# A two-layer decoder trunk on one core: the adaptive norms' parameters computed at other places, and an overflow branch moved

## The chip, the core and the metric

The kernel runs on one core of a Trainium2 chip. Five engines work side by side, each in its own order: TensorE (PE in the profile) multiplies matrices, VectorE (DVE) and ScalarE (ACT) work element by element, GpSimd (POOL) does little here, and SyncE (SP) issues the transfers from memory. The metric is the device time of one execution in microseconds; before the change its median is 909.39 us over 3 runs (909.15 to 909.47).

## What is computed

256 tokens of 1024 features pass through two layers. Each layer has a token mixer and a channel mixer, and each of the four sub-layers is wrapped in an adaptive norm whose parameters come from one vector c.

```python
def adaln_params(c, w, b):
    m = jax.nn.silu(c) @ w + b
    shift, scale, gate = jnp.split(m, 3, axis=-1)
    return shift[:, None, :], scale[:, None, :], gate[:, None, :]
...
    for i in range(DEPTH):
        shift, scale, gate = adaln_params(c, ada_w[i, 0], ada_b[i, 0])
        h = x * (1.0 + scale) + shift
        if i % N_MIXERS == 0:
            y = stick_breaking_attention(h, sb_w_in[i // 2], sb_w_out[i // 2])
        else:
            y = retention(h, positions, ret_w_in[i // 2], ret_gn_g[i // 2], ret_w_out[i // 2])
        x = layer_norm(DEEPNORM_ALPHA * x + (1.0 + gate) * y, ln_g[i, 0], ln_b[i, 0])
        shift, scale, gate = adaln_params(c, ada_w[i, 1], ada_b[i, 1])
        h = x * (1.0 + scale) + shift
        y = grouped_moe(h, router_w, router_b, moe_w_gate[i], moe_w_up[i], moe_w_down[i])
        x = layer_norm(DEEPNORM_ALPHA * x + (1.0 + gate) * y, ln_g[i, 1], ln_b[i, 1])
```

Layer 0 mixes tokens by stick-breaking attention (16 heads of 64), layer 1 by retention. The channel mixer routes every token to 2 of 16 experts; each expert computes silu(t @ w_gate) * (t @ w_up) @ w_down with 512 hidden features. All weights are float32: ada_w holds 4 x 1024 x 3072 of them, the experts of one layer 16 x 3 x 1024 x 512.

## The kernel before

**Stages.** The program runs through attention (the phase called STICK, 0 to about 207 us), the experts of layer 0 (SPARSE, to about 443 us), retention (RETEN, to about 660 us), the experts of layer 1 and the last norm. Nearly all bytes are weights. They come in tiles of 1 MB over one queue: SyncE issues them in program order into a ring of places, and an issue waits until the earlier owner of its place has been read. So a transfer that stands early in that order delays all behind it.

**Precision.** In the attention and retention products each float32 tile is split into a rounded part and a remainder (ScalarE L382, VectorE L383), and each product is three matmuls (L403 to L405). In the expert stages the matmuls take float32 as it is (L969 for gate and up, L1086 for down).

**Adaptive norms.** The parameters of sub-layer i are six parts j of 512 columns (shift 0 and 1, scale 2 and 3, gate 4 and 5). A part needs two ada_w tiles and is made in `ada_part`, on TensorE (L277) or by one multiply and seven multiply-adds on VectorE (L280, L282). Its rest, a turn into columns by four small matmuls (L292) and an addition of the bias (L293), comes later. `plan(i, js, on_pe)` puts parts on a list, each `fill()` finishes the last part and begins the next, `flush()` works the list off.

```python
    plan(0, range(4), on_pe=True)
...
    plan(2, range(1))
    plan(2, range(1, 4), on_pe=True)
```

**The start.** Four parts of norm 0 are made on TensorE, with the small tables (`vectors()`, L200 to L210) queued behind the first two tiles. Then x comes, is transposed (L448), shaped by the norm and split (`modulated`), and the dense products of q, k and v for the first half of the heads begin. `stick_attn` follows per pair of heads: z (L616, L617), a mask (DVE L619), three activations (ACT L621 to L623), a sum over keys on TensorE (L627, L628), an exponential (L630) and the product with v (L634, L635).

**The step to the experts.** After the output product of the attention layer come the logits of the router (L335, L343), the choice of experts, and the first gather of tokens (L940). In the program the last three parts of norm 2 stand between the output product and the logits.

**The experts.** Experts are worked in 8 pairs p: `up` for gate and up, `spread`, the gather of the next pair, the down products, and a scatter back (L1062) that is held over to the next pair. Each pair needs 12 tiles. An expert has room for a fixed number of tokens; `spill` handles those that overflow, inside a branch (L862) that all engines test and that is not taken with this input. It stands at the end of pair 1, behind the held scatter.

**The order.** Within each engine instructions run in a fixed order that a scheduler lays down when the program is built, from priorities (`urgent()` raises them) and from `tc.issue_after`; `behind(work)` puts work after the last matmul noted. On the chip an engine never passes over an instruction that waits.

## Time and profile before

| | |
|---|---|
| median of 3 runs | 909.39 us |
| the profiled execution: its own time, its span | 911.27 us, 909.6 us |
| TensorE busy | 854.3 us (94%) |
| VectorE busy | 500.6 us (55%) |
| ScalarE busy | 278.4 us (31%) |
| bytes moved | 310.05 MB, 341 GB/s over the span |

The profiled execution is one execution of the program. Its own time is 1.7 us above its span and 1.9 us above the median of the runs. A busy share is a mean over stages with different limits, so stages are read one by one: by windows, by the order of the instructions, and by who waited for whom.

### The profile page before, as it was taken

How to read it: one execution, taken by the hardware profiler on the slowest of the kernel's cores; microseconds unless marked ns; L12 is line 12 of the kernel's file. 1: busy time of each engine (PE TensorE's matmuls, PEld its weight loads, DVE VectorE, ACT ScalarE, POOL GpSimd, SP SyncE). 2: the span in 40 equal slices, each digit the busy share in tenths (PEclk: the TensorE clock that was granted, in tenths of full speed). 3: DMA queues.
4: the chain of work that ended last, by engine and by line, in shares of the span. 5: the costliest groups of instructions: out<-in, count | busy, mean ns of one | idle time of the engine just before them, and what ended most of it. 6: DMA issues, size and time to landing. Idle time of an engine off the chain costs nothing. (4 is left out here: it accounts for less than half of the span.)

```text
span 909.6 us, 11176 instructions
## 1 busy us (share of the span) xinstructions
PE 854.3 (94%) x4345; PEld 525.2 (58%) x4345; DVE 500.6 (55%) x943; ACT 278.4 (31%) x395; POOL 25.3 (3%) x46
## 2 busy tenths in 40 slices
...
GB/s 303 385 387 387 340 327 318 274 410 213 418 413 411 419 419 415 416 418 390 198 218 365 305 301 212 340 147 310 291 182 402 415 417 418 414 417 419 418 335 46
DMA packets 90035, 310.05 MB, mean 341 GB/s; under 512 B 5652, under 2 KB 6092, under 8 KB 73588
## 3 DMA queue, kind: packets, MB, share of 16 engines
...
HBM read 308.17 MB, written 1.05 MB: 340 GB/s over the span
## 5 line engine op out<-in xcount | busy, mean ns | idle before, releaser
L969 PE MATMUL ps<-s,xg 128*64 128x512 f32 x632 | 168.2, 595 | 2.2 <-DVEq L862 1.4
L969 PE MATMUL ps<-w,xg 128*64 128x512 f32 x392 | 111.7, 604 | 6.4 <-PEq L862 6.4
L969 PEld LDWEIGHTS ps<-s,xg 128*64 128x64 f32 x632 | 52.9, 137 | 86.5 <-issue 80.3
L1086 PE MATMUL ps<-w,hidT 128*64 128x512 f32 (+1 forms) x296 | 83.6, 574 | 0.1
L382 ACT ACTIVATE wp<-w 128x1024 fp32r<-128x1024 f32 x57 | 59.9, 1057 | 65.9 <-PE ps L405 59.4
L383 DVE TENSOR_TENSOR wp<-w,wp 128x1024 fp32r<-128x1024 f32 x57 | 69.3, 1218 | 18.2 <-ACT wp L382 18.2
L1019 DVE TENSOR_TENSOR mosg<-mosg,ps 128x512 f32<-128x512 f32 x16 | 11.0, 687 | 117.4 <-PE ps L969 117.4
L969 PEld LDWEIGHTS ps<-w,xg 128*64 128x64 f32 x392 | 35.7, 139 | 62.7 <-issue 60.7
L1086 PE MATMUL ps<-s,hidT 128*64 128x512 f32 (+1 forms) x248 | 71.8, 568 | 0.0
L282 DVE SCALAR_TENSOR_TENSOR s<-w,cact,s 128x512 f32<-128x512 f32 x88 | 65.6, 745 | 0.7
L1051 DVE SCALAR_TENSOR_TENSOR moy<-ps,cs,gate 128x512 f32<-128x512 f32 (+1 forms) x34 | 24.3, 716 | 71.8 <-PE ps L1086 71.8
L382 ACT ACTIVATE moyh<-moy 128x512 fp32r<-128x512 f32 (+1 forms) x34 | 20.6, 605 | 124.1 <-DVE moy L1051 124.1
L404 PE MATMUL ps<-wp,hh 128*128 128x512 f32 (+1 forms) x144 | 56.2, 392 | 0.0
L405 PE MATMUL ps<-wp,hl 128*128 128x512 f32 x144 | 55.5, 390 | 0.0
L454 ACT ACTIVATE xg<-ps,mod 128x256 f32<-128x256 f32 x32 | 17.8, 563 | 121.1 <-PE ps L940 121.1
L403 PE MATMUL ps<-wp,hh 128*128 128x512 f32 (+1 forms) x144 | 53.7, 393 | 0.6 <-ACT hh L382 0.6
L1067 DVE TENSOR_TENSOR res<-res,ps 128x512 f32<-128x512 f32 x48 | 30.4, 682 | 37.6 <-PE ps L1062 37.1
L1086 PEld LDWEIGHTS ps<-w,hidT 128*64 128x64 f32 x296 | 27.4, 136 | 33.9 <-issue 30.9
L1017 ACT ACTIVATE mosg<-ps 128x512 f32<-128x512 f32 x16 | 9.5, 596 | 112.3 <-PE ps L969 112.3
L1086 PEld LDWEIGHTS ps<-s,hidT 128*64 128x64 f32 x248 | 24.8, 137 | 29.9 <-issue 28.5
L403 PE MATMUL ps<-s,wp 128*128 128x256 f32 x128 | 37.6, 297 | 0.6 <-DVE fcol L222 0.6
L404 PE MATMUL ps<-s,wp 128*128 128x256 f32 x128 | 37.1, 293 | 0.0
(344 smaller groups left out, 1532.6 us busy)
## 6 DMA issues: line engine op xcount, KB each, us to landing
s<-in_moe_w_up SPq DMA_DIRECT2D x45, 1024.0 KB, 15.1
w<-in_ada_w SPq DMA_DIRECT2D x39, 1024.0 KB, 7.6
w<-in_moe_w_down SPq DMA_DIRECT2D x35, 1024.0 KB, 13.4
s<-in_moe_w_gate SPq DMA_DIRECT2D x34, 1024.0 KB, 11.6
w<-in_moe_w_gate SPq DMA_DIRECT2D x30, 1024.0 KB, 15.1
s<-in_moe_w_down SPq DMA_DIRECT2D x29, 1024.0 KB, 17.0
w<-in_moe_w_up SPq DMA_DIRECT2D x19, 1024.0 KB, 16.3
w<-in_ret_w_in SPq DMA_DIRECT2D x18, 1024.0 KB, 6.9
```

Of the source, the lines that this page charges most:

```text
L282: V.scalar_tensor_tensor(e, wt[:, kk, :], cact[:, k:k + 1], e, op0=OP.mult, op1=OP.add)
L382: A.activation(hi, src, AF.Copy)
L383: return V.tensor_tensor(lo, src, hi, op=OP.subtract).ins
L403: T.matmul(dst, lh, rh, start=start, stop=False)
L404: T.matmul(dst, lh, rl, start=False, stop=False)
L405: state["mm"] = T.matmul(dst, ll, rh, start=False, stop=stop).ins
L454: return A.activation(dst, src, AF.Identity, scale=sc[:, k:k + 1], bias=sh[:, k:k + 1]).ins
L969: state["mm"] = T.matmul(o[64 * u:64 * u + 64, :], xg[:, k, at:at + CAP], ts[u][kk], start=(k == 0), stop=(k == NK - 1)).ins
L1019: V.tensor_tensor(sgt, sgt, pu, op=OP.mult)
L1051: V.scalar_tensor_tensor(y, py, cs, gate[:, c0:c0 + n], op0=OP.mult, op1=OP.mult)
L1067: V.tensor_tensor(r, r, sos[b], op=OP.add)
L1086: state["mm"] = T.matmul(py[64 * u:64 * u + 64, :], hidT[:, f, u * CAP:(u + 1) * CAP], ts[h][u][:, i, c0:c0 + n], start=(f == 0), stop=(f ...
```

## The change

Four things change. First, norm 0 is made in two halves of the features: parts 0 and 2 and half of x come first, the first halves of the q and k products run on them (`feat_part`), and parts 1 and 3, the other half of x and the second halves follow. The small tables (`vectors()`, `folded_vectors()`, `aux`) are loaded behind that, out of `small_loads`; positions and router_b come as rows and are turned by TensorE. Second, the four parts of norm 2 leave the attention stage: they are planned for the expert stage of layer 0, one `fill()` after each of the pairs 1 to 5, all on VectorE. Third, `spill` moves from the end of pair 1 to the middle of pair 0 in both expert stages, and the expert tiles are loaded by `fetch` in an order of their own, 18 of them ahead of the branch. Fourth, in the expert stage the gathers and the last down products are put behind the last matmul noted, and the last moments become urgent.

```diff
...
 SLOTS = 8
+AHEAD = 18
...
-       "SPARSE": {"xs": (4, 1024), "xq": (2, 2048), "t2": (6, 512), "oneh": (2, 512), "pc": (1, 256), "pt": (2, 256)}}
+       "SPARSE": {"xs": (4, 1024), "xq": (2, 2048), "t2": (6, 512), "oneh": (2, 512), "pc": (1, 256), "pt": (2, 256), "E": (1, 512)}}
 HIGH = {"STICK": {"hA": (0, 1), "qz": ((2, 0), (3, 0)), "k4": ((4, 0), (4, 1024), (5, 0), (5, 1024)),
...
     A.activation(cact, colp[:, 0:8], AF.Silu)
+    col = keep([P, 176], "col")
+    adac = ps()
+    T.transpose(adac[:, 0:96], rows[0:96, 0, :], ident[0:96, 0:96])
+    V.tensor_copy(col[:, 0:96], adac[:, 0:96])
     part = keep([P, 2], "part")
...
         SY.dma_start(rows[64:80, 1, :], ret_gn_g[0].rearrange("(k p) -> k p", p=P))
         cq = ps()
-        T.transpose(cq[:, 0:96], rows[0:96, 0, :], ident[0:96, 0:96])
-        T.transpose(cq[:, 96:176], rows[0:80, 1, :], ident[0:80, 0:80])
-        V.tensor_copy(col, cq[:, 0:176])
+        T.transpose(cq[:, 0:80], rows[0:80, 1, :], ident[0:80, 0:80])
+        V.tensor_copy(col[:, 96:176], cq[:, 0:80])
         SY.dma_start(con[:, 2 * P:_KEPT], const[:, 2 * P:_KEPT])
-        SY.dma_start(posi, positions[0].rearrange("(b p) -> p b", p=P))
+        prow = big([P, 2, P], "rows")
+        posr = prow[0:NB, 0, :].bitcast(I32)
+        SY.dma_start(posr, positions[0].rearrange("(b p) -> b p", p=P))
+        SY.dma_start(prow[0:1, 1, 0:NE], router_b.rearrange("(o e) -> o e", o=1))
         SY.dma_start(wr.rearrange("p (t q) e -> p t q e", q=4), router_w.rearrange("(t p q) e -> p t q e", p=P, q=4))
-        SY.dma_start(rb, router_b.rearrange("(o e) -> o e", o=1).to_broadcast([P, NE]))
+        pr = ps()
+        prf = big([P, P], "crow")[0:NB, :]
+        V.tensor_copy(prf, posr)
+        T.transpose(pr[:, 0:NB], prf, ident[0:NB, 0:NB])
+        T.matmul(pr[:, NB:NB + NE], ones[0:1, :], prow[0:1, 1, 0:NE], start=True, stop=True)
+        V.tensor_copy(posi, pr[:, 0:NB])
+        V.tensor_copy(rb, pr[:, NB:NB + NE])
         V.tensor_copy(counts[:, 0, :], C["strict"])
...
-            for kk, wh, wl in pieces(w[kt * 512:(kt + 1) * 512, j * 512:(j + 1) * 512]):
-                k = 4 * kt + kk
-                for m in range(4):
-                    mm3(out_ps[m // 2][:, m % 2, :], wh[:, m * P:(m + 1) * P], wl[:, m * P:(m + 1) * P],
-                        hh[:, k, :], hl[:, k, :], k == 0 and m % 2 == 0, k == NK - 1 and m % 2 == 1)
+    def feat_part(out_ps, hh, hl, w, j, kt, amid=None):
+        for kk, wh, wl in pieces(w[kt * 512:(kt + 1) * 512, j * 512:(j + 1) * 512]):
+            k = 4 * kt + kk
+            if kk == 2 and amid:
+                amid()
+            for m in range(4):
+                mm3(out_ps[m // 2][:, m % 2, :], wh[:, m * P:(m + 1) * P], wl[:, m * P:(m + 1) * P],
+                    hh[:, k, :], hl[:, k, :], k == 0 and m % 2 == 0, k == NK - 1 and m % 2 == 1)
...
-        def whole(w, p, kt):
-            return [[t[:, f, :] for f in range(4)] for t in
-                    (load(w[l, 2 * p + u, 512 * kt:512 * kt + 512, :].rearrange("(p f) c -> p (f c)", p=P), None)
-                     for u in range(2))]
+        tiles, order = {}, [(w, p, h, u) for p in range(NE // 2) for w in range(3) for h in range(2) for u in range(2)]
+
+        def fetch(key=None, n=0):
+
+            while (key is not None and key not in tiles) or len(tiles) < n:
+                w, p, h, u = order[len(tiles)]
+                e = 2 * p + u
+                tiles[w, p, h, u] = load(moe_w_down[l, e, 256 * h:256 * h + 256, :], shape=(P, 2, 1024)) if w == 2 else \
+                    load((moe_w_gate, moe_w_up)[w][l, e, 512 * h:512 * h + 512, :].rearrange("(p f) c -> p (f c)", p=P), None)
+            return tiles.get(key)
...
                 held.pop(0)()
             sgt = big([P, 512], "mosg")
             A.activation(sgt, pg, AF.Silu)
-            pu = up(moe_w_up, p, xg, 1, up(moe_w_up, p, xg, 0))
+            pu = up(1, p, xg, 1, up(1, p, xg, 0))
             V.tensor_tensor(sgt, sgt, pu, op=OP.mult)
+            if p == 0:
+                fetch(n=AHEAD)
+                spill(l, xh, xl, sc, sh, over, flag, gate)
             pt, cs = spread(p, oneh)
...
-            if ahead:
+            if ahead and p:
+                behind(lambda: gather(nxt, 2 * (p % 2)))
+            elif ahead:
...
                         down(py, c0, w, h)
                 for py, (c0, w) in zip(pys, blocks):
                     weighed(py, c0, w)
-            if p == 1:
-                while held:
-                    held.pop(0)()
-                spill(l, xh, xl, sc, sh, over, flag, gate)
             after(p)
-    plan(0, range(4), on_pe=True)
+
+    def banks(tag):
+        t = ps([P, 2, 512], tag)
+        return [t[:, u, :].rearrange("p (m s) -> p m s", m=2) for u in range(2)]
+
+    plan(0, (0, 2), on_pe=True)
     fill()
-    vectors()
-    fill(2)
-    SY.dma_start(res, xrows)
-    aux = big([P, 5 * P], "aux")
+    SY.dma_start(res[:, :, 0:512], xrows[:, :, 0:512])
     fill()
-    SY.dma_start(aux, const[:, _KEPT:])
+    xT = banks("px")
+    for k2 in range(2):
+        transposed([res[:, b, :] for b in range(NB)], k2, xT[k2])
     flush()
     sc, sh = ada_mod(0)
-    hh, hl, _ = modulated([res[:, b, :] for b in range(NB)], sc, sh)
+    hh = big([P, NK, S], "hh", F32R)
+    hl = big([P, NK, S], "hl", F32R)
+
+    def shape_half(half, tps):
+        for k2, tp in zip((2 * half, 2 * half + 1), tps):
+            h = big([P, 2, S], "hm")
+            for q in range(2):
+                shaped(h[:, q, :], tp[:, q, :], sc, sh, 2 * k2 + q)
+            split_to(hh[:, 2 * k2:2 * k2 + 2, :], hl[:, 2 * k2:2 * k2 + 2, :], h)
+
+    shape_half(0, xT)
+    q0, k0 = banks("pz"), banks("px")
+    plan(0, (1, 3), on_pe=True)
+    feat_part(q0, hh, hl, sb_w_in[0], 0, 0)
+    SY.dma_start(res[:, :, 512:1024], xrows[:, :, 512:1024])
+    fill()
+    feat_part(k0, hh, hl, sb_w_in[0], 2, 0, fill)
+    xT = [transposed([res[:, b, :] for b in range(NB)], k2) for k2 in (2, 3)]
+    with urgent():
+        flush()
+        shape_half(1, xT)
     A.activation(res, res, AF.Copy, scale=ALPHA)
-    folded_vectors()
+    aux = big([P, 5 * P], "aux")
     plan(0, range(4, 6))
     plan(1, range(6))
-    plan(2, range(1))
-    plan(2, range(1, 4), on_pe=True)
     oh = big([P, NK, S], "oh", F32R)
     ol = big([P, NK, S], "ol", F32R)
+
+    def tables():
+        if small_loads:
+            small_loads.pop(0)()
+        fill()
+
+    small_loads = [lambda: SY.dma_start(aux, const[:, _KEPT:]), lambda: (vectors(), folded_vectors())]
     for half in range(2):
-        qkv = stick_in(hh, hl, half, fill)
+        qkv = stick_in(hh, hl, half, fill if half else tables, *(() if half else (q0, k0)))
         stick_attn(oh, ol, aux, *qkv, half)
     fill(2)
     gate = gate_row(0)
...
     st = stats_tiles(4)
-    moe(0, 1, xs, sc, sh, L, st, lambda p: rotary_tables() if p == 4 else None)
+    plan(2, range(4))
+    moe(0, 1, xs, sc, sh, L, st, lambda p: rotary_tables() if p == 6 else fill() if p else None)
+    flush()
     phase("RETEN", "second")
...
     moe(1, 3, xs, sc, sh, L, st, lambda p: rows_.append(ln_rows(3)) if p == NE // 2 - 1 else None)
-    for b, (m, r) in enumerate(both_moments(st)):
+    with urgent():
+        ends = both_moments(st)
+    for b, (m, r) in enumerate(ends):
```

VectorE in the attention stage, at the place where the norm's last features are shaped; before (L453 shapes them into s_207 and s_135, the L383 row with s_201 splits them, L282 works on a part of another norm):

```order
L280 TENSOR_SCALAR s_82<-s_376,cact 128x512
L282 SCALAR_TENSOR_TENSOR s_82<-s_376,cact,s_82 128x512
L453 TENSOR_SCALAR s_207<-ps_221,sums_101 128x256
L282 SCALAR_TENSOR_TENSOR s_82<-s_376,cact,s_82 128x512
L453 TENSOR_SCALAR s_135<-ps_230,sums_101 128x256
L282 SCALAR_TENSOR_TENSOR s_82<-s_376,cact,s_82 128x512
L383 TENSOR_TENSOR s_201<-s_207,s_200 128x512
L282 SCALAR_TENSOR_TENSOR s_82<-w_382,cact,s_82 128x512
L383 TENSOR_TENSOR s_201<-s_135,s_200 128x512
L383 TENSOR_TENSOR wp_314<-lo_312,wp_314 128x1024
```

And now, where L470 is the shaping of the second half of the features, L291 and L293 a part of another norm, L223, L209 and L218 copies of small tables, and L304 and L307 the end of part 3 of norm 0:

```order
L291 TENSOR_SCALAR s_82<-w_413,cact 128x512
L394 TENSOR_TENSOR wp_377<-s_348,wp_377 128x1024
L293 SCALAR_TENSOR_TENSOR s_82<-w_413,cact,s_82 128x512
L304 TENSOR_TENSOR sums_104<-ps_327,col 128x4
L223 CAST counts<-con 128x128
L293 SCALAR_TENSOR_TENSOR s_82<-w_413,cact,s_82 128x512
L307 TENSOR_SCALAR sums_104<-sums_104 128x4
L209 COPY col<-ps_488 128x80
L293 SCALAR_TENSOR_TENSOR s_82<-w_413,cact,s_82 128x512
L218 CAST s_159<-s_159 2x128
L470 TENSOR_SCALAR s_159<-ps_317,sums_104 128x256
L293 SCALAR_TENSOR_TENSOR s_82<-w_419,cact,s_82 128x512
```

The shaping of the second half now stands behind the copies of the small tables and four steps of another norm's part.

TensorE in the attention stage, where the product for v (ps_525 and ps_526, in three rows each) begins; before, z of the first pair of heads is pz_615:

```order
L403 MATMUL ps_525<-wp_529,s_200 128x512
L404 MATMUL ps_525<-wp_529,s_200 128x512
L405 MATMUL ps_525<-wp_529,s_201 128x512
L403 MATMUL ps_525<-wp_529,s_200 128x512
L404 MATMUL ps_525<-wp_529,s_200 128x512
L405 MATMUL ps_525<-wp_529,s_201 128x512
L616 MATMUL pz_615<-s_251,s_253 128x256
L617 MATMUL pz_615<-s_251,s_253 128x128
L616 MATMUL pz_615<-s_251,s_253 128x256
L617 MATMUL pz_615<-s_251,s_253 128x128
L403 MATMUL ps_526<-wp_529,s_200 128x512
L404 MATMUL ps_526<-wp_529,s_200 128x512
```

And now, where z of the third pair is pz_669, the sum over keys of the first pair is px_631 (L644, L645), L233 turns the vectors loaded late, and the product for v is ps_531:

```order
L633 MATMUL pz_669<-s_345,s_347 128x256
L634 MATMUL pz_669<-s_345,s_347 128x128
L633 MATMUL pz_669<-s_345,s_347 128x256
L634 MATMUL pz_669<-s_345,s_347 128x128
L644 MATMUL px_631<-s_82,s_126 128x384
L645 MATMUL px_631<-s_82,s_126 128x128
L644 MATMUL px_631<-s_82,s_126 128x384
L645 MATMUL px_631<-s_82,s_126 128x128
L233 MATMUL ps_506<-con,s_126 128x40 x4
L303 MATMUL ps_512<-con,s_82 128x2 x4
L414 MATMUL ps_531<-wp_535,s_157 128x512
L415 MATMUL ps_531<-wp_535,s_157 128x512
```

Three z, the first sum over keys and L233 now stand ahead of the product for v; before, v and z alternated.

TensorE at the end of the attention stage; before, from the last output product (po_1341) to the last part of norm 2, with the router's transposes at L335:

```order
L405 MATMUL po_1341<-s_1355,ol_250 128x256
L335 MATMUL pz_1511<-con,res 128x128 x4
L292 MATMUL ps_1440<-con,s_82 128x2 x4
L277 MATMUL ps_1446<-lo_1447,cact 32x512 x4
L277 MATMUL ps_1446<-s_1453,cact 32x512 x4
L292 MATMUL ps_1460<-part,s_135 128x2 x4
L277 MATMUL ps_1466<-w_1467,cact 32x512 x4
L277 MATMUL ps_1466<-w_1473,cact 32x512 x4
L292 MATMUL ps_1480<-part,s_82 128x2 x4
L277 MATMUL ps_1487<-w_1488,cact 32x512 x4
L277 MATMUL ps_1487<-w_1494,cact 32x512 x4
L292 MATMUL ps_1501<-part,s_135 128x2
```

And now, from the last output product (po_1334), with the transposes at L346 and the logits at L354:

```order
L414 MATMUL po_1334<-s_1348,oh_343 128x256
L415 MATMUL po_1334<-s_1348,oh_343 128x256
L416 MATMUL po_1334<-s_1348,ol_344 128x256
L346 MATMUL ps_1434<-con,res 128x128 x4
L346 MATMUL ps_1435<-con,res 128x128 x4
L346 MATMUL pz_1436<-con,res 128x128 x4
L346 MATMUL ps_1437<-con,res 128x128 x4
L354 MATMUL px_1433<-ws_1322,l_1439 128x16 x4
L354 MATMUL px_1433<-ws_1322,s_126 128x16 x4
```

The six rows of L277 and the L292 rows between are gone from this place, and the transposes follow the output product directly.

## Rows read from the trace of the kernel before

**Rows 1.** The head of the page: the span, and busy time, share of the span and instructions of each engine.

```profile
span 909.6 us, 11176 instructions
...
PE 854.3 (94%) x4345; PEld 525.2 (58%) x4345; DVE 500.6 (55%) x943; ACT 278.4 (31%) x395; POOL 25.3 (3%) x46
```

**Rows 2.** Who waited for whom on TensorE: tile and line that waited, what it waited for, us in total, times, longest.

```profile
PE ps L277 <- DMA w<-in_ada_w: 8.1, 7, 4.0
PE ps L969 <- PEq L862: 6.4, 1, 6.4
PE ps L292 <- ACT s L287: 5.0, 7, 0.8
...
PE ps L969 <- DVEq L862: 1.4, 1, 1.4
```

**Rows 3.** Busy time of each engine in stretches of the span: the stretch, its length, then busy us (and instructions) of each engine, the granted clock as a share of 2.4 GHz, the mean share of the 16 DMA engines, GB/s.

```profile
20.00:41.80 21.80, 16.06 (x80) 8.97 (x77) 5.38 (x12) 7.19 (x10) 0.00 (x0) 0.58 1.05 386
...
54.00:72.00 18.00, 17.47 (x138) 16.91 (x137) 14.41 (x23) 9.11 (x14) 0.00 (x0) 1.00 1.05 386
72.00:90.40 18.40, 18.40 (x100) 15.27 (x98) 16.05 (x23) 14.48 (x15) 0.00 (x0) 1.00 1.05 387
...
100.00:140.00 40.00, 40.00 (x273) 35.11 (x272) 35.23 (x53) 25.12 (x35) 0.00 (x0) 1.00 0.92 325
140.00:180.50 40.50, 39.97 (x230) 32.01 (x229) 37.67 (x69) 19.89 (x25) 0.55 (x1) 1.00 0.77 283
...
273.00:439.00 166.00, 161.83 (x742) 67.06 (x738) 53.49 (x119) 17.55 (x32) 0.00 (x0) 0.99 1.00 402
```

**Rows 4.** TensorE in order of time at the start: start, us, instruction, idle time before it and what ended that.

```profile
7.40 1.93 PE L277 MATMUL ps<-w,cact 128*32 128x512 f32 x8 [3.95 <-DMA w<-in_ada_w]
...
34.27 1.87 PE L292 MATMUL ps<-part,s 128*128 128x2 f32 x8 [0.78 <-ACT s L287]
...
41.80 0.55 PE L403 MATMUL ps<-s,wp 128*128 128x256 f32 x1 [0.64 <-DVE fcol L222]
```

**Rows 5.** TensorE in order of time from the last product of the attention layer (L405) to the first expert matmul (L969).

```profile
180.16 0.28 PE L405 MATMUL po<-s,ol 128*128 128x256 f32 x1
...
184.35 1.05 PE L292 MATMUL ps<-part,s 128*128 128x2 f32 x8 [0.78 <-ACT s L287]
...
191.65 0.38 PE L292 MATMUL ps<-part,s 128*128 128x2 f32 x2 [0.78 <-ACT s L287]
...
210.14 1.08 PE L969 MATMUL ps<-s,xg 128*64 128x512 f32 x4 [0.42 <-ACT xg L454]
```

**Rows 6.** The same stretch of the second layer, from the last product of the retention layer to the first expert matmul.

```profile
659.60 0.28 PE L405 MATMUL po<-s,hl 128*128 128x256 f32 x1
...
674.55 0.65 PE L969 MATMUL ps<-s,xg 128*64 128x512 f32 x2 [0.41 <-ACT xg L454]
```

**Rows 7.** VectorE groups from 0 to 207 us: line, operation, names, shapes, count, busy us, mean ns of one, idle before.

```profile
L282 DVE SCALAR_TENSOR_TENSOR s<-w,cact,s 128x512 f32<-128x512 f32 x46 | 34.3, 745 | 0.4
L383 DVE TENSOR_TENSOR wp<-w,wp 128x1024 fp32r<-128x1024 f32 x22 | 26.8, 1220 | 7.5 <-ACT wp L382 7.5
...
L619 DVE TENSOR_TENSOR s<-pz,s 128x768 f32<-128x768 f32 x8 | 7.6, 948 | 0.0
...
L453 DVE TENSOR_SCALAR s<-ps,sums 128x256 f32<-128x256 f32 x4 | 2.1, 536 | 0.0
...
L212 DVE CAST counts<-con 128x128 bf16<-128x128 f32 x1 | 1.6, 1570 | 3.0 <-DMA con<-in_const 3.0
```

**Rows 8.** ScalarE in order of time in the first pair of heads.

```profile
75.07 0.83 ACT L621 ACTIVATE s<-s 128x768 f32<-128x768 f32 x1
75.92 1.28 ACT L622 ACT_TABLE_LOAD   x1
77.21 0.85 ACT L622 ACTIVATE s<-s 128x768 f32<-128x768 f32 x1
78.08 1.28 ACT L623 ACT_TABLE_LOAD   x1
```

**Rows 9.** TensorE in order of time: the first product for the second half of the heads.

```profile
87.38 0.36 PE L403 MATMUL ps<-s,wp 128*128 128x256 f32 x1
```

**Rows 10.** TensorE around the overflow branch of the first expert stage.

```profile
264.02 0.73 PE L1062 MATMUL ps<-moyh,pt 128*128 128x512 f32 x2 [0.59 <-ACT moyh L382]
265.17 0.73 PE L1062 MATMUL ps<-moyl,pt 128*128 128x512 f32 x2 [0.42 <-DVE moyl L383]
272.26 1.12 PE L969 MATMUL ps<-w,xg 128*64 128x512 f32 x2 [6.36 <-PEq L862]
```

**Rows 11.** DMA from 400 to 440 us: GB/s in 40 slices of 1 us, and the weights of the next stage that were issued in it.

```profile
GB/s 426 385 442 410 414 410 406 406 414 401 410 414 414 397 410 414 406 399 399 387 389 381 391 385 387 387 385 389 385 385 381 281 100 8 90 360 403 211 0 0
...
w<-in_ret_w_in SPq DMA_DIRECT2D x6, 1024.0 KB, 14.3
```

**Rows 12.** TensorE in the last down products of the first expert stage.

```profile
430.56 0.81 PE L1086 MATMUL ps<-w,hidT 128*64 128x256 f32 x2
...
438.95 0.38 PE L1086 MATMUL ps<-w,hidT 128*64 128x256 f32 x1
```

**Rows 13.** DMA from 865 to 895 us, near the end of the second expert stage: GB/s in 40 slices of 0.75 us.

```profile
GB/s 393 470 393 437 393 410 404 426 404 393 437 399 393 431 399 388 410 426 404 393 431 382 328 246 66 22 0 0 0 0 0 0 0 0 0 0 0 0 0 0
```

42 lines of the change are left out of this document (19 added, 23 removed).

## The prediction

> **What bounds the kernel now.** I read the page's head first: TensorE is busy 854.3 of 909.6 us [rows 1]. Its list of waits is short: 8.1 us for ada_w tiles, 6.4 us at the overflow branch of the first expert stage, 5.0 us for ScalarE inside the adaptive-norm parts, 1.4 us at the other branch [rows 2]. So time is gained where TensorE does something that could lie elsewhere, or runs slowly, and lost wherever a new wait opens. The windows tell the second half of the story [rows 3]: from 72 to 180.5 us TensorE is 97 to 100% busy, but VectorE is busy 16.05 of 18.40 us and then 37.67 of 40.50, so the attention stage has little room on VectorE; and the expert stage moves 402 GB/s over 166 us, so it has little room in the transfers. These two are what the change leans on. A difference below 0.2%, 1.8 us, can't be told from no change here.
>
> **The start.** The first dense matmul begins at 41.80, behind four parts of norm 0; until then the granted clock is 0.58 in the mean from 20 us on, mostly the lower of its two levels [rows 3, 4]. Now only two parts stand ahead of it. By SyncE's new order 0.2 MB of small tiles, four ada_w tiles, half of x and the first sb_w_in tile come before it, 6 MB in all. The stream begins about 4.0 (the first ada_w tile is used at 7.40, less 1.2 MB at 386 GB/s, and 0.3 for the landing) [rows 3, 4]; 6 MB end at about 20, and splits, shaping and the halves of x follow, so the first dense matmul comes at about 26. That is 15.5 us earlier, but parts 1 and 3 then stand among the dense products. A part costs 2 x 1.93 of multiplying and 1.87 of its rest at the low clock [rows 4], about 6 for two at the upper level with the wait for ScalarE. Without new waits the gain is 9.
>
> **What stands against that gain.** The second halves of q and k need the second half of x shaped, and VectorE does this in order. The place shown from VectorE puts a multiply on tile w_413 ahead of it. About 13.3 tiles of 1.05 MB precede that tile's end on the queue: 14.0 MB at 386 GB/s is 36.2, from 4.0, so 40 to 41. From there VectorE does a split (1.22), a cast (1.57), seven steps of multiply kind (0.745 each, 5.2), two shapings, two short splits and six small ones (about 3.4 together, an estimate from the other rows): 11.4, up to 52 [rows 7]. TensorE has finished the first halves and the transposes by then and idles some 8 to 10 us.
>
> From 52 to the first product of the second half of the heads (87.38 before [rows 9]) VectorE has, by its new order, 22 steps of multiply kind (16.4), seven splits (8.5), eight steps of attention kind at 0.95 (7.6) and small ones (2.7): 35.2, or 32 as steps begin some 0.08 before the last one ends. With no wait it is through at 84, 3 us earlier than before. But it waits. The second q product must be copied by ScalarE before k's next split (about 3). Then the first two pairs' activations run one behind the other: each pair is 0.83, a table load of 1.28, 0.85, another load of 1.28 and 0.85 [rows 8], 5.1, of which VectorE covers 0.95 with the other pair's mask, so twice 4. Before, the loads came twice and a third loaded table served the rest; the new ScalarE order has five ahead of it. And in this stretch TensorE has nothing to fill with, because the product for v stands behind the first sum over keys (the second place shown). Waits of 3, 4 and 4 and the rest give 97, which is 9 to 10 late; with the lower clock after the idle stretch up to 12. The Trainium skill (ScalarE: Activation LUTs, What ACT_TABLE_LOAD costs) adds a drain of 1.38 us to every load of 1.28. The trace shows none: the activation begins 1.29 after the load [rows 8]; by the page the five loads would take 6.9 us more and this term would be past its upper bound.
>
> So the ends are -9 (no new wait) and +12. If VectorE is as busy as before in such stretches, 0.80 to 0.87 (14.41 of 18.00, 16.05 of 18.40 [rows 3]), its 32 us take 37 to 40 and end at 89 to 92. That row is the nearest, and I take **+4** for the attention stage. It isn't made up later, since TensorE is full from there to 180 [rows 3]; one part less on VectorE (6 us) only keeps it from growing.
>
> **The step to the experts.** Between the last output product and the first expert matmul lie 29.98 us (180.16 to 210.14), with three parts of norm 2 at 180.8 to 192 and their waits for ScalarE of 0.78 each [rows 5]. The same stretch of the second layer, without such parts, takes 14.95 (659.60 to 674.55) [rows 6]. The difference is 15.0. Part of the stretch may now wait for VectorE or ScalarE instead, so -13 to -16; I take **-15**. Norm 2 isn't needed until retention, so nothing else is late.
>
> **The first expert stage.** It gains 0.59 and 0.42 of waits for the scatter ahead of the branch, about -1 [rows 10]. The branch itself stays: 6.36 of idle time before, and 1.40 in the second layer [rows 2, 10]. What sets the one or the other the trace doesn't tell, so at the new place it may cost 1.4 to 6.4. The Trainium skill (Runtime: NRT & Kernel Launch, Instruction fetch mechanics) says that a taken branch whose target lies outside the fetched pages stalls until they are fetched; jumping over the branch's body is such a case wherever it stands, so by that rule nothing is saved, against 5 us if pair 0 gave it the short price. I count nothing. The four rests add 4 x 8 small matmuls, 0.95 to 1.05 each, +4.
>
> The transfers matter more. Eight ada_w tiles join the stage's queue: 8 x 1.049 MB at 410 GB/s is 20.5 us. From 400 to 440 us no expert tile is issued, only tiles of the next stage, with 14.3 us from issue to landing; so the last expert tile lands at about 416 [rows 11]. Its first use is at about 430.6 and the last down products end at 439.2 [rows 12]. The room is 15, so the last tiles come 5 to 6 late against the same first expert matmul, and TensorE's gain of 1 is hidden: +6 by the transfers, +3 less up to 5 by TensorE alone. The later of the two decides; if the queue gets further ahead before the stage, it is less. Ends -3 and +7; I take **+4**. Retention's weights then land later too, but the transfers pause between 432 and 436 [rows 11].
>
> **The second expert stage.** No tiles are added. The branch and its scatter waits are worth at most 2.4, at worst the branch costs more; the transfers end there at about 882 [rows 13], near the end of the stage, so little of a gain passes. **-1**, from -2.4 to +3.
>
> **Sum.** 4 - 15 + 4 - 1 = -8. The profiled execution takes 911.27, 1.7 more than its span [rows 1], so 903.3 for it; it is 1.9 above the median, so 901.4 as a median, I say 901. The first bounds alone give 879 to 917.
>
> **The rivals.** (1) The start has no new waits: VectorE finds other work ready and the product for v comes on time. For it: VectorE's sum alone ends at 84. Against it: the two places in the order. -9 - 15 + 4 - 1 = -21, so 888. (2) Slower, by the product for v: TensorE idles behind the last shaping and again behind the chain of mask, activations and sum over keys, so that the second half of the heads begins 15 us late, and the clock falls in these gaps. -13 with +4 and +0 then leave +6 over: 15 - 13 + 4 + 0 = 6, so 915. It decides against the change from the point at which that product begins later than 87.4 + 12, at 99.5. For it: the sum with its waits gives 97 already, without the clock. Against it: that sum takes every wait in full. (3) The expert stage's transfers take more back: +7 for +4, and the queue is also late for retention, +3: 907; it can't undo 15 by itself. That the parts moved don't leave the path is excluded by the third place of the order.
>
> **How the numbers follow.** The forecast has 0.45 and a range of its own of 893 to 907; rival 1 has 0.22, rival 2 0.23, rival 3 0.10. The range of 8 in 10 goes from 886 to 916. Faster by over 0.2% come nine tenths of the forecast (0.40), rival 1 (0.22) and half of rival 3 (0.05): 0.67. Within 0.2% lie some hundredths of the forecast's upper end, of rival 3 and of rival 2's lower end: 0.07. The rest, most of it rival 2, is slower: 0.26.
>
> **What would show it.** The first dense matmul near 26; a gap of TensorE from about 41 to 52 that ends on VectorE; the first product of the second half between 89 and 97; 15 us from the last output product to the first expert matmul; late tiles, as waits of L992 (the new line of the up products) for transfers, in the last pair of the first expert stage. It is wrong if the second half begins before 84 or after 99, if the expert stage shows no wait for transfers, or if the branch costs TensorE more than 7 us in pair 0.

## The result, and the profile after

The change makes the kernel slower: 919.99 us (median of 4 runs, 917.58 to 924.51) against 909.36 us for the kernel before in the same batch (909.15 to 909.47). The ratio is 1.0123, with a 95% interval of 1.0097 to 1.0148. The forecast was 901, and its range ended at 916.

The head of the page of the changed kernel, to be held against [rows 1]:

```profile
span 917.0 us, 11099 instructions
...
PE 845.2 (92%) x4300; PEld 520.2 (57%) x4300; DVE 519.0 (57%) x970; ACT 281.3 (31%) x395; POOL 25.4 (3%) x46
```

The span grew by 7.4 us although TensorE is busy 9.1 us less. So it stands idle 16.5 us longer. (The 7.4 are the difference of two single executions; between the medians it is 10.6, since the profiled execution of the kernel before took 1.9 us more than its median and this one 0.6 less.) The list of its waits, answering to [rows 2], says for what (what waited, for what, us in total, times, longest):

```profile
PE ps L288 <- DMA w<-in_ada_w: 7.0, 3, 3.3
PE ps L957 <- PEq L879: 6.2, 1, 6.2
PE ps L1090 <- ACT moyh L393: 5.6, 5, 2.7
PE ps L957 <- issue: 4.4, 1, 4.4
PE ps L992 <- DMA s<-in_moe_w_up: 4.0, 1, 4.0
...
PE pz L633 <- DVE s L636: 2.4, 2, 1.4
...
PE px L644 <- DVE s L641: 2.0, 1, 2.0
```

The branch (L879) costs 6.2 in the first expert stage, as before. In the second, where it cost 1.4, there is now a stop of 4.4; it comes five matmuls behind the branch, the profile names nothing that ended it, and it is put down to the branch here because no_branch (below) has no such stop. New are an expert tile that comes 4.0 late and waits for VectorE in the first pair of heads. Where the time went is seen best by cutting the span at six moments of TensorE: the start of its last product of each layer's mixer, of the first expert matmul of each layer and of the first product of retention, and the end of its last matmul. The table holds the lengths between them in us (the experiments' rows are used below). Each row is one profiled execution, and such executions differ: that of spill_only took 4.2 us more than its median, and spill_only, loads8 and no_branch, whose attention stage is the same code, end it at 180.6, 178.1 and 177.2. So a difference of 2 or 3 us in this table says nothing by itself.

| | to the last attention product | to the experts | first expert stage | retention | to the experts | second expert stage |
|---|---|---|---|---|---|---|
| before | 180.2 | 30.0 | 239.9 | 209.5 | 15.0 | 223.8 |
| after | 190.2 | 15.0 | 251.8 | 210.4 | 14.6 | 223.5 |
| spill_only | 180.6 | 30.0 | 226.1 | 210.6 | 16.6 | 225.6 |
| norm2_back | 191.3 | 29.2 | 225.6 | 210.5 | 14.9 | 224.9 |
| norm2_only | 180.2 | 15.0 | 250.1 | 210.4 | 16.6 | 230.1 |
| start_old | 180.3 | 15.0 | 250.0 | 210.4 | 16.6 | 224.9 |
| loads8 | 178.1 | 26.8 | 247.2 | 210.5 | 16.6 | 224.5 |

After against before: +10.0, -15.0, +11.9, +0.9, -0.4, -0.3.

**The attention stage.** TensorE of the changed kernel in order of time, the answer to [rows 4] (start, us, instruction, idle time before it and what ended that): first dense product, the tables' turns, first product on the second half of the features.

```profile
25.67 0.58 PE L414 MATMUL pz<-s,wp 128*128 128x256 f32 x1
...
46.13 0.34 PE L208 MATMUL ps<-con,s 80*128 80x80 f32 x1 [1.42 <-DVE sums L304]
...
47.93 0.26 PE L219 MATMUL ps<-con,s 2*128 2x2 f32 x1 [1.46 <-DVE s L218]
...
49.05 0.58 PE L414 MATMUL pz<-s,wp 128*128 128x256 f32 x1 [0.40 <-ACT s L393]
...
50.91 0.58 PE L415 MATMUL pz<-s,wp 128*128 128x256 f32 x1 [1.28 <-DVE s L394]
```

The dense products begin 16.1 us earlier than before, and then TensorE waits 4.6 us in four pieces until it has the second half of x. The windows of the changed kernel (stretch, length, busy us of PE, PEld, DVE, ACT and POOL with their instructions, granted clock, DMA share, GB/s) answer to [rows 3]:

```profile
42.00:54.00 12.00, 7.43 (x44) 6.64 (x43) 10.28 (x22) 5.25 (x6) 0.00 (x0) 0.68 1.03 364
54.00:72.00 18.00, 13.82 (x96) 12.90 (x95) 11.52 (x16) 7.94 (x13) 0.00 (x0) 0.93 1.05 386
72.00:90.40 18.40, 15.37 (x82) 12.45 (x81) 10.67 (x17) 13.54 (x14) 0.00 (x0) 1.00 0.88 310
100.00:140.00 40.00, 40.00 (x291) 35.64 (x290) 33.55 (x50) 26.27 (x36) 0.00 (x0) 1.00 0.75 264
```

From 54 to 72 TensorE was busy 17.47 us and is now busy 13.82; from 72 to 90.4 it was 18.40 and is 15.37. VectorE is not the fuller for it: 10.67 us in the last stretch against 16.05. It waits too, as its own order of time shows in the first two pairs of heads (L641 needs the third activation, L640):

```profile
76.39 0.96 DVE L641 SCALAR_TENSOR_TENSOR s<-s 128x768 f32<-128x768 f32 x1 [2.60 <-ACT s L640]
81.44 0.96 DVE L641 SCALAR_TENSOR_TENSOR s<-s 128x768 f32<-128x768 f32 x1 [4.09 <-ACT s L640]
```

ScalarE is what they wait for. From 71.2 to 82.7 it works without a pause, and in that time it loads a table five times (1.28 us each):

```profile
72.07 1.28 ACT L639 ACT_TABLE_LOAD   x1
73.36 0.84 ACT L639 ACTIVATE s<-s 128x768 f32<-128x768 f32 x1
74.22 1.28 ACT L640 ACT_TABLE_LOAD   x1
...
77.11 1.28 ACT L639 ACT_TABLE_LOAD   x1
...
79.27 1.28 ACT L640 ACT_TABLE_LOAD   x1
...
81.42 1.28 ACT L647 ACT_TABLE_LOAD   x1
```

The first product of the second half of the heads, at 87.38 before [rows 9], starts at 96.69, 9.3 us late:

```profile
96.69 0.28 PE L414 MATMUL ps<-s,wp 128*128 128x256 f32 x1
```

From 100 on TensorE is full again (40.00 of 40.00), so the delay stays: the stage ends 10.0 late. From the first dense product to the last output product, before and after, the windows are:

```profile
41.80:180.16 138.36, 136.81 (x874) 118.96 (x874) 122.66 (x190) 78.96 (x102) 0.55 (x1) 0.98 0.93 339
```

```profile
25.67:190.16 164.49, 148.79 (x934) 127.67 (x930) 121.29 (x192) 86.66 (x108) 0.55 (x1) 0.95 0.85 306
```

The stretch begins 16.1 earlier and is 26.1 longer: 14.1 of that is idle time (15.70 for 1.55) and 12.0 busy time, among it the two parts of norm 0 that now lie in it, and the granted clock is lower (0.95 for 0.98).

**The step to the experts** is what the forecast said, 15.00 us from the last output product to the first expert matmul, with the transposes (L346) directly behind:

```profile
190.16 0.28 PE L416 MATMUL po<-s,ol 128*128 128x256 f32 x1
190.28 1.13 PE L346 MATMUL ps<-con,res 128*128 128x128 f32 x8
...
205.16 1.08 PE L992 MATMUL ps<-s,xg 128*64 128x512 f32 x4 [0.42 <-ACT xg L471]
```

**The first expert stage.** TensorE's long stops in it are the branch and two expert tiles:

```profile
229.14 1.19 PE L957 MATMUL ps<-oneh,xh 128*128 128x256 f32 x4 [6.24 <-PEq L879]
...
367.53 1.07 PE L992 MATMUL ps<-w,xg 128*64 128x512 f32 x2 [0.78 <-DMA w<-in_moe_w_up]
372.58 1.11 PE L992 MATMUL ps<-s,xg 128*64 128x512 f32 x1 [3.98 <-DMA s<-in_moe_w_up]
```

And from 400 to 440 us, where before only tiles of the next stage were issued [rows 11], expert tiles still are (from the list of issues: destination and source, queue, count, KB each, median us to landing where it lies in the stretch):

```profile
w<-in_moe_w_up SPq DMA_DIRECT2D x4, 1024.0 KB, 20.2
w<-in_moe_w_down SPq DMA_DIRECT2D x2, 1024.0 KB
s<-in_moe_w_down SPq DMA_DIRECT2D x2, 1024.0 KB
```

### The profile page after: what moved, and what is told of

It reads as the page before. It is cut to its first block, busy times and chain, and to the rows that moved or that the text cites. A ratio compares the mean times of both kernels' runs of the same rounds, so it can differ in the third digit from the quotient of the medians.

```text
span 917.0 us, 11099 instructions
## 1 busy us (share of the span) xinstructions
PE 845.2 (92%) x4300; PEld 520.2 (57%) x4300; DVE 519.0 (57%) x970; ACT 281.3 (31%) x395; POOL 25.4 (3%) x46
## 5 line engine op out<-in xcount | busy, mean ns | idle before, releaser
L992 PE MATMUL ps<-s,xg 128*64 128x512 f32 x584 | 159.3, 599 | 4.8 <-DMA s<-in_moe_w_up 4.0
L992 PE MATMUL ps<-w,xg 128*64 128x512 f32 x440 | 126.6, 600 | 0.8 <-DMA w<-in_moe_w_up 0.8
L992 PEld LDWEIGHTS ps<-s,xg 128*64 128x64 f32 x584 | 49.4, 138 | 91.3 <-issue 80.9
L1113 PE MATMUL ps<-s,hidT 128*64 128x512 f32 (+1 forms) x272 | 75.5, 570 | 0.0
L1113 PE MATMUL ps<-w,hidT 128*64 128x512 f32 (+1 forms) x272 | 74.3, 575 | 0.0
L992 PEld LDWEIGHTS ps<-w,xg 128*64 128x64 f32 x440 | 38.7, 138 | 59.0 <-issue 55.6
L293 DVE SCALAR_TENSOR_TENSOR s<-w,cact,s 128x512 f32<-128x512 f32 x84 | 62.8, 747 | 0.9
L1113 PEld LDWEIGHTS ps<-w,hidT 128*64 128x64 f32 x272 | 23.9, 138 | 28.7 <-issue 26.5
L957 PE MATMUL ps<-oneh,xh 128*128 128x256 f32 x128 | 24.1, 313 | 8.9 <-PEq L879 6.2
L394 DVE TENSOR_TENSOR moyl<-moy,moyh 128x512 fp32r<-128x512 f32 (+1 forms) x34 | 22.4, 659 | 15.8 <-ACT moyh L393 15.7
## 6 DMA issues: line engine op xcount, KB each, us to landing
w<-in_ada_w SPq DMA_DIRECT2D x35, 1024.0 KB, 10.6
s<-in_moe_w_gate SPq DMA_DIRECT2D x30, 1024.0 KB, 11.8
```

The costliest lines, as they stand in the source:

```text
L293: V.scalar_tensor_tensor(e, wt[:, kk, :], cact[:, k:k + 1], e, op0=OP.mult, op1=OP.add)
L394: return V.tensor_tensor(lo, src, hi, op=OP.subtract).ins
L957: T.matmul(gp[:, kk, :], part[b][:, k * P:(k + 1) * P], oneh[:, b].rearrange("p e s -> p (e s)"), start=(n == 0), stop=(n == len(steps) - 1))
L992: state["mm"] = T.matmul(o[64 * u:64 * u + 64, :], xg[:, k, at:at + CAP], ts[u][:, kk, :], start=(k == 0), stop=(k == NK - 1)).ins
L1113: state["mm"] = T.matmul(py[64 * u:64 * u + 64, :], hidT[:, f, u * CAP:(u + 1) * CAP], ts[h][u][:, i, c0:c0 + n], start=(f == 0), stop=(f ...
```

## The experiments

All ratios are against the kernel before, run beside it on the same chip. The quoted expectations were written before each run; letters in them are the names that theories had then, and the text here names them in words.

### Which of the parts costs

norm2_back is the changed kernel with norm 2 back in the attention stage:

```diff
+    plan(2, range(1))
+    plan(2, range(1, 4), on_pe=True)
...
-    plan(2, range(4))
-    moe(0, 1, ..., lambda p: rotary_tables() if p == 6 else fill() if p else None)
-    flush()
+    moe(0, 1, ..., lambda p: rotary_tables() if p == 4 else None)
```

> The changed kernel with norm 2 again at its old place (the start in halves and the branch in pair 0 stay). Theory A (the start loses 10 us through VectorE's order, norm 2's tiles lose 12 us in the first expert stage, the branch loses nothing there): last output product again near 190, 30 us from there to the first expert matmul, first expert stage back to about 240 us from first up product to first retention product, total 917 to 921. Rival B (the expert stage lost its 12 us through the early branch and the new fetch order, not through norm 2's tiles): the stage stays at 248 to 252, total 927 to 931.

norm2_only is the kernel before with the opposite edit (and with the tile E that the parts need there, paid for by a smaller scratch for transfers, 2048 for 4096, as in the change):

> The kernel before with norm 2's four parts in the first expert stage and nothing else. Theory A: 15 us less to the first expert matmul, which comes near 195; the transfers then bind the stage, their pause of some 10 us ahead of it closes, the last expert tile lands near 427, and 6 to 9 us of the 15 are given back: total 900 to 905. Rival B: the tiles fit, only the small matmuls are added, total 896 to 898.

spill_only is the kernel before with the new expert function: `fetch`, the branch in pair 0, gathers and last down products behind the last matmul, urgent last moments.

> The kernel before with the new expert function alone (branch in pair 0, fetch order, behind) and the urgent last moments; norm 2 at its old place, start as before. Theory A: 907 to 911, the branch still costs 6 in the first stage and 1.4 to 4.5 in the second. Rival B: the first expert stage is 8 us or more longer, total 916 or more.

start_old is spill_only with norm 2 in the expert stage, so all of the change but the start.

> The changed kernel with the start of before (norm 0 in one piece, small tables early); norm 2 in the expert stage, branch in pair 0. Theory A: last output product near 180, first expert matmul near 195, the expert stage bound by its transfers, so of the 10 us only a part comes through: total 902 to 910. Rival C (the 10 us of the start pass to the end in full, the expert stage has the same length as in the changed kernel): 908 to 911 with a stage of 252. Rival B: as C.

Measured: norm2_back 909.79 us, 0.9993 (0.9974 to 1.0013); norm2_only 915.85, 1.0058 (1.0041 to 1.0074); spill_only 898.49, 0.9853 (0.9837 to 0.9870); start_old 909.48, 0.9991 (0.9975 to 1.0006); before 910.12. So the new expert function gains 11.6. On top of it the start costs 11.3 (norm2_back less spill_only), and norm 2 in the expert stage costs 11.0 (start_old less spill_only). -11.6 + 11.3 + 11.0 = 10.7, and 10.6 was measured: counted on top of the function the parts add up, and two of three do harm. Counted from the kernel before they don't: norm 2 alone costs 5.7 (norm2_only), and the function on top of it gains 6.4 and not 11.6 (start_old less norm2_only). The table says where. Moving norm 2 gives back 15.0 ahead of the experts and takes 23.9 in them (226.1 to 250.0; 5.65 of it is the branch, which stops TensorE for 6.35 us in start_old and for 0.70 in spill_only). In norm2_only it takes 10.2 there, and the second expert stage, which the edit doesn't touch, is 6.3 longer: the stop at the branch in it went from 1.40 to 6.01. The new expert function shortens the first expert stage by 13.8. The expectations missed the totals of the first three: norm2_back and spill_only came out faster than any of their theories, norm2_only slower. The total of start_old lies in the ranges of two theories; its stage of 250.0 speaks for the one by which the start's loss passes to the end in full.

### What fills the first expert stage

no_branch leaves out the handling of overflow, and with it the branch, in both expert stages:

```diff
             if p == 0:
                 fetch(n=AHEAD)
-                spill(l, xh, xl, sc, sh, over, flag, gate)
```

> The kernel spill_only without the overflow branch: the handling of overflowing tokens is left out in both layers (with this input it isn't entered). If the branch costs what the idle times behind it show (0.7 in the first stage, 6.2 in the second, and 1 to 2 for the lower clock after it): 889 to 892. If the engines would have idled there anyway: 896 to 899.

loads8 is spill_only with eight more ada_w tiles in the queue, two after each of the pairs 1 to 4, of which VectorE reads one element each:

```diff
+    def extra(p):
+        if 0 < p < 5:
+            for kt in range(2):
+                wt = load(ada_w[1, 0, kt * 512:(kt + 1) * 512, p * 512 - 512:p * 512])
+                V.tensor_copy(junk, wt[:, 3, 511:512])
```

> The kernel spill_only with eight more 1 MB tiles of ada_w loaded in the first expert stage, two after each of the pairs 1 to 4, one element of each read on VectorE and used for nothing; norm 2 at its old place. Theory A (the tiles alone make the stage longer): the stage from first up product to first retention product grows from 226 to 242 to 247, total 914 to 920. Rival D (VectorE's multiplies and the small matmuls on TensorE do it): within 3 us of spill_only.

Measured: no_branch 889.61, 0.9792 (0.9749 to 0.9834); loads8 919.31, 1.0109 (1.0079 to 1.0139); before 909.65. The branch costs some 9 us of spill_only's time in both stages together (the four runs of no_branch spread from 886.85 to 892.40). The eight transfers alone, without a single product of the norm, cost 20.8 us against spill_only, nearly all of it in the first expert stage (226.1 to 247.2). 8 x 1.049 MB at 410 GB/s are 20.5: none of it is hidden. The list of TensorE's waits in that stage is headed by late expert tiles:

```profile
PE ps L976 <- DMA s<-in_moe_w_gate: 6.9, 2, 4.3
...
PE ps L976 <- DMA s<-in_moe_w_up: 4.8, 4, 1.3
...
PE ps L976 <- DMA w<-in_moe_w_gate: 2.2, 2, 1.3
```

Why spill_only has no room for them is seen from the issue of its last expert tile and the time from there to its landing (last figure, us). First the kernel before, then spill_only:

```profile
397.10 1.76 SPq L165 DMA_DIRECT2D w<-in_moe_w_down  x1
w<-in_moe_w_down SPq DMA_DIRECT2D x1, 1024.0 KB, 20.8
```

```profile
398.27 1.08 SPq L166 DMA_DIRECT2D w<-in_moe_w_down  x1
w<-in_moe_w_down SPq DMA_DIRECT2D x1, 1024.0 KB, 20.1
```

The tile lands at 417.9 and at 418.4, the same date, though TensorE is through with the stage 13.4 us earlier in spill_only. The last pair's down products begin at 429.0 before, 11 us behind that landing, and at 416.7 in spill_only, ahead of it: no room is left. With norm 2's tiles in the queue the last expert tile lands at 424.6 (norm2_only) and 428.3 (start_old), though the first expert matmul comes 15 us earlier.

The waits are not all that is lost. The first expert stage of loads8, of spill_only and of the changed kernel, one after the other, as windows with the columns above:

```profile
204.90:452.10 247.20, 226.99 (x1042) 95.25 (x1042) 91.87 (x207) 36.15 (x62) 0.70 (x1) 0.98 1.00 401
```

```profile
210.60:436.60 226.00, 218.78 (x1042) 95.00 (x1043) 91.51 (x199) 36.08 (x62) 0.70 (x1) 0.99 1.00 403
```

```profile
205.20:456.90 251.70, 232.17 (x1074) 98.49 (x1074) 113.70 (x240) 36.02 (x62) 0.70 (x1) 0.97 0.99 395
```

loads8 has the same matmuls as spill_only, and they take 8.2 us longer. TensorE works at the lower level of its clock, 1.2 GHz, for 10.1 us of the stage and for 3.0 in spill_only; at half the clock this is some 3.5 of the 8.2, an estimate. What makes the rest is not shown. The stage of the changed kernel is 25.7 longer than that of spill_only: 12.3 of it is idle time (19.5 against 7.2), of which the branch makes 5.5 and the late tiles 4.8, and 13.4 is busy time, of which the norm's 32 small matmuls make 4.2. Of the other 9.2 some 5 go with the clock, by the same estimate: TensorE works at the lower level for 12.9 us of this stage and for 3.0 of spill_only's, most of it from 227.2 to 234.0, behind the branch's stop, and from 370.6 to 377.4, behind the stop for tiles. What makes the last 4 is not shown. In loads8 the tiles come on top of all others, while in the changed kernel they leave the queue ahead of the stage, so 20.8 is an upper bound for what they cost there.

branch_back is spill_only with the branch at its old place, the end of pair 1.

> spill_only with the branch at its old place behind the held scatters at the end of pair 1; fetch order, behind and urgent moments stay. Theory G (the branch's place makes most of the 14 us that the first expert stage gained): the stage back at 234 to 240, total 905 to 910. Rival H (the order of the gathers behind the last matmul and of the fetches makes it): the stage at 226 to 230, total 898 to 902.

Measured: 901.29, 0.9906 (0.9881 to 0.9931), before 910.82. The first expert stage takes 233.8: of spill_only's 13.8 us the place of the branch makes 7.7 in this program (its stop is 6.38 here and 0.70 there), and the new order of loads, gathers and last products 6.1. The total fits the rival theory, the stage lies between both. In the second stage the old place is the better one, 219.4 against 225.6.

### What holds up the attention stage

tables_late and no_fill are norm2_back with less work in the first half of the heads. In the one the small tables come at the start of the second half; in the other the parts of other norms do.

```diff
-    small_loads = [lambda: SY.dma_start(aux, const[:, _KEPT:]), lambda: (vectors(), folded_vectors())]
+    small_loads = [lambda: SY.dma_start(aux, const[:, _KEPT:])]
     for half in range(2):
+        if half:
+            vectors()
+            folded_vectors()
```

> norm2_back with the small tables and the turned vectors loaded only before the second half of the heads; their copies on VectorE leave the place ahead of the shaping, and the product for v is then built in between the z products again. Theory A1 (the 11 us of the start come from the product for v standing behind the first sum over keys, which the late tables bring about): last output product at 181 to 185, total 899 to 904. Rival A2 (they come from the parts of norms on VectorE ahead of the shaping and of the splits): no change, 190 to 192 and 908 to 912.

```diff
     def tables():
         if small_loads:
             small_loads.pop(0)()
-        fill()
...
-        qkv = stick_in(hh, hl, half, fill if half else tables, ...)
+        qkv = stick_in(hh, hl, half, (lambda: fill(2)) if half else tables, ...)
```

> norm2_back without any part of a norm begun in the first half of the heads; they follow two at a time in the second half. Theory A1: the second half of the features is shaped some 3 us earlier, but the product for v stays behind the z products and the work comes back later on VectorE: last output product at 188 to 196, total 906 to 916. Rival A2: last output product at 180 to 184, total 898 to 904.

halves_only is norm2_back with the tables loaded early, as before; tables_only is norm2_back with norm 0 made in one piece, as before.

> norm2_back with the small tables loaded as early as in the kernel before (behind the first two ada_w tiles) and the turned vectors behind the first halves: norm 0 in halves without the tables behind it. Theory E (the halves themselves are worth the 9 us of the earlier first product, and the tables queued behind them cost 20): last output product at 170 to 177, total 886 to 897. Rival F (the halves leave VectorE's chain as it is, TensorE only waits later, whatever the tables do): last output product at 186 to 196, total 905 to 915.

> spill_only with norm 0 in one piece as before, and only the small tables, aux and the turned vectors queued behind as in the change. Theory E: the tables put the attention of the first heads ahead of v, last output product at 188 to 200, total 906 to 918. Rival F: the tables do no harm by themselves, last output product at 177 to 182, total 895 to 900.

Measured: tables_late 916.32, 1.0066 (1.0045 to 1.0088); no_fill 921.06, 1.0131 (1.0099 to 1.0164); halves_only 911.74, 1.0017 (1.0005 to 1.0029); tables_only 902.73, 0.9900 (0.9865 to 0.9934). Held against 898.49 for spill_only, the two halves cost 13 us with the tables early and 11 with them late; the tables alone cost 4 (their interval touches that of spill_only, 0.9837 to 0.9870). So it is the halves. tables_late and no_fill came out slower than any of their theories. In no_fill, with fewer parts on VectorE, the second half of the heads does begin 5.7 us earlier (92.8 against 98.5 in norm2_back), and the stage ends 10.9 later (202.2 against 191.3): the parts then stand where TensorE had been full, and its idle time from 85 us to the end of the stage rises from 1.6 to 9.7. In tables_late TensorE idles less from 42 to 85 (6.6 us for 12.1), but the second half only begins at 113.0: bringing the tables nearer to their use makes it worse.

v_first raises the product for v in halves_only; gate_on_pe makes parts 4 and 5 of norm 0 on TensorE; both joins the two.

```diff
-        for b, t in enumerate(dense_tok(hh, hl, w, 4 + half)):
+        with (nullcontext() if half else urgent()):
+            vt = dense_tok(hh, hl, w, 4 + half)
+        for b, t in enumerate(vt):
...
-    plan(0, range(4, 6))
+    plan(0, range(4, 6), on_pe=True)
```

> halves_only with the product for v of the first half made urgent, so that it is built in ahead of the z products of the first heads. Theory V (the place of v costs the 10 us): last output product at 178 to 184, total 897 to 904. Rival W (VectorE's parts of norms in that stretch cost them): 188 to 194 as in halves_only.

> halves_only with parts 4 and 5 of norm 0 made on TensorE, which takes 12 us of multiplies from VectorE in the first half of the heads and adds some 6 to TensorE. Theory V: 190 to 198 for the last output product. Rival W: 178 to 186.

> halves_only with the product for v urgent and parts 4 and 5 of norm 0 on TensorE. Theory V: like v_first, later by up to 6 (184 to 190). Rival W: like gate_on_pe, 178 to 186. If both are needed: under 178.

z_after_v puts the first z behind the product for v by force:

```diff
+            with (tc.issue_after(hold) if half == 0 and m == 0 else nullcontext()):
```

> halves_only with the first z product made to follow the whole product for v (v_first had left the order as it was, since v's banks wait for the rest of a norm's part). Theory V (the place of v costs the 10 us): the idle time of TensorE from 42 to 85 us falls from 12 to 6 or less, last output product at 180 to 186, total 898 to 905. Rival X (in halves TensorE reaches the same chain of VectorE and ScalarE earlier and waits there in whichever order): 188 to 196, total 907 to 916.

Measured: v_first 911.23, 0.9987 (0.9958 to 1.0016); gate_on_pe 913.54, 1.0035 (1.0012 to 1.0058); both 924.35, 1.0155 (1.0126 to 1.0185); z_after_v 912.94, 1.0028 (1.0004 to 1.0052).

v_first tells nothing of v's place: the product for v stayed behind the z and the sum over keys of the first heads (it begins at 82.4, in halves_only at 81.9). Its stage ends at 194.2 even so, 3.9 later than that of halves_only. The clock can make all of this: TensorE works at the lower level for 17.2 us of v_first's stage and for 5.6 of the other, which at half the clock is 5.8, an estimate.

z_after_v does change the order, and the chain of activations leaves the stretch from 70 to 85. Here halves_only, and then z_after_v, in that window:

```profile
70.00:85.00 15.00, 10.62 (x56) 8.49 (x55) 6.65 (x9) 12.05 (x12) 0.00 (x0) 1.00 1.05 380
```

```profile
70.00:85.00 15.00, 10.21 (x37) 8.41 (x36) 8.84 (x16) 1.32 (x2) 0.00 (x0) 0.66 1.05 380
```

ScalarE falls from 12.05 to 1.32 us, and TensorE is no busier. The second half begins 4.2 earlier (93.5 against 97.7), the stage ends 5.6 later (195.9 against 190.3). But the run is no clean test of v's place, for two reasons. TensorE meets a new stop just ahead of v, at the turn of the late vectors, which waits for their transfer:

```profile
75.23 0.68 PE L233 MATMUL ps<-con,s 40*128 40x40 f32 x4 [4.79 <-DMA s<-in_ln_b]
```

Without these 4.79 its idle time from 42 to 85, 11.6 us, would be 6.8, near the 6 that the theory of v's place asked for. And the granted clock is 0.66 in the window shown, for 1.00: TensorE works at the lower level for 21.7 us of the stage and for 5.6 in halves_only, which at half the clock is some 8 us, an estimate, and more than the 5.6 by which the stage ends later. So whether the chain of table loads ahead of v decides, or only shows, stays open.

VectorE's load does not decide: with gate_on_pe VectorE is busy 3.88 us of the 16 from 54 to 70 (halves_only 11.20), and TensorE's idle time from 42 to 85 is 11.0. It is 11.8 in the changed kernel, 12.1 in norm2_back, 12.0 in halves_only, 11.6 in z_after_v, and 1.0 before. Nor are the transfers what TensorE waits for there: in the changed kernel each of its waits from 42 to 85 ends on ScalarE or VectorE, none on a tile. The reading that fits is that TensorE arrives up to 16 us earlier at work whose splits, masks and activations keep their pace, and waits for one or the other of them; no run shows this by itself. That is as far as the runs go; no single wait was found whose removal gives the time back.

Of the expectations only those of halves_only (the halves don't help) and z_after_v (188 to 196) held in both figures, and gate_on_pe fits the theory of v's place with 196.0; v_first ends its stage just past the range of its rival, tables_only lies between its two theories, and the run called both missed its own. Much of what it takes more than gate_on_pe is the branch: its stop in the second expert stage is 6.19, there 0.50.

### What the branch costs

pad puts 64 small matmuls ahead of the second expert stage of spill_only, to move the branch's place in the instructions. branch_mixed leaves the branch in pair 0 in the first expert stage and at the end of pair 1 in the second.

> spill_only with 64 more small matmuls on TensorE just ahead of the second expert stage, of no use. If the price of the branch follows where the code lies in memory: the idle time behind the branch in the second stage moves away from 6.2, to anything between 0.5 and 6.5, while the first stage's stays at 0.7. If it follows what surrounds the branch: 6.2 again.

```diff
-            if p == 0:
+            if p == 0 and l == 0:
                 fetch(n=AHEAD)
                 spill(l, xh, xl, sc, sh, over, flag, gate)
...
+            if p == 1 and l == 1:
+                while held:
+                    held.pop(0)()
+                spill(l, xh, xl, sc, sh, over, flag, gate)
             after(p)
```

> spill_only with the branch in pair 0 in the first expert stage and at the end of pair 1 in the second, each where it was cheapest so far (0.7 and 1.4). If the prices go with those places: first stage 226, second 219, total 891 to 894. If they don't: 897 to 904.

Measured: pad 920.96, 1.0118 (1.0047 to 1.0189); branch_mixed 892.75, 0.9792 (0.9748 to 0.9836). In pad the stop in the second stage stayed at 6.2 and that in the first at 0.7, and the edit cost over 20 us elsewhere, for a reason that was not sought, so it says only that 64 instructions more don't move the price. branch_mixed puts each branch where it was cheap: spill_only has these stops,

```profile
229.03 0.71 PE L941 MATMUL ps<-oneh,xh 128*128 128x256 f32 x4 [0.70 <-PEq L863]
...
687.75 0.55 PE L941 MATMUL ps<-oneh,xh 128*128 128x256 f32 x1 [6.15 <-PEq L863]
```

and branch_mixed has the first of them and, in the second stage, this one:

```profile
720.96 1.98 PE L976 MATMUL ps<-s,xg 128*64 128x512 f32 x4 [1.40 <-DVEq L863]
```

The second expert stage falls from 225.6 to 219.1. At 892.75 us branch_mixed is the fastest version that computes everything, 17 us below the kernel before and 27 below the changed one: the change's expert function with a branch moved once instead of twice, and without its start and its place for norm 2.

## Why the prediction was wrong

The forecast was 4 - 15 + 4 - 1 = -8. Measured by the stages: +10.0, -15.0, +11.9, -0.3, and +0.8 in the rest of the span. The start lies within its bounds (up to +12), the first expert stage beyond its own (up to +7). Its upper bounds, +12 - 13 + 7 + 3 = +9, make 918 and not the 917 that was said, and 919.99 is past both.

**The start, +4: wrong in the choice, right in the working.** The first dense matmul came at 25.67 (about 26 was said), VectorE split the shaped second half by 51.4 (up to 52), and the first product of the second half at 96.7 (97 by the sum with its waits). Two sizes in it were off and partly cancel: the cast of a small table was counted at 1.57 and took 0.22, and the wait for tile w_413 ended at 41.98 instead of 40 to 41. From 51.45 to 96.69 VectorE is busy 30.92 us (32 was said) and waits 14.3 (11 was said). TensorE's idle time behind the first halves was 4.6 and not 8 to 10. The step that failed is "That row is the nearest, and I take +4": it set the sum of the waits aside for VectorE's busy share before the change, 0.80 to 0.87. In the changed kernel that share is 10.67 of 18.40, 0.58, because VectorE now waits for ScalarE and TensorE. A busy share of the kernel before can't hold waits that the change brings; the two waits for ScalarE, forecast as twice 4, were 2.60 and 4.09. The Trainium skill (ScalarE: Activation LUTs, What ACT_TABLE_LOAD costs) would put a drain of 1.38 us on each table load. None shows here either: the load at 72.07 takes 1.28, and its activation starts at 73.36. What brings the waits about, the halves apart, stays open.

**The product for v (the slower rival).** The second half of the heads began at 96.7, short of the 99.5 from which that rival decides. Its other claim, that the chain in front of v is the cause, was not settled by z_after_v. Its total of 915 is nearer to the measured time than the forecast, but its terms are not: it had the start at +15 and the first expert stage at +4.

**The step to the experts, -15: right**, 15.0.

**The first expert stage, +4: wrong.** The small matmuls cost the 4.2 that was said, and the branch in pair 0 kept its price (6.24 after 6.36), so counting nothing for it was right in this program, by luck: at the same place it costs 0.70 in spill_only. The Trainium skill (Runtime: NRT & Kernel Launch, Instruction fetch mechanics) says that a taken branch whose target isn't in the fetched pages waits for their fetch. The prediction took the jump over the branch's body for such a case wherever it stands; 6.24 fits that, 0.70 doesn't, and no run shows where the target lay. The step that failed is the one on the transfers, "The room is 15, so the last tiles come 5 to 6 late against the same first expert matmul", and with it "The later of the two decides". The room was counted from a first expert matmul at 210, but that matmul was to come earlier by the 15 us of the step ahead of it, and the tiles did not land earlier for that: in norm2_only, where the first expert matmul comes at 195.2, the last expert tile lands 6.7 us later than before (424.6 for 417.9), and the stage is 10.2 longer. The same 15 us were spent twice. In the changed kernel the late tiles cost 4.8 of waiting, in the sixth pair and not in the last as was said, with the clock at its lower level behind it, beside the 4.2. And the -1 for the rest of the expert function was far too small: alone it takes 13.8 off that stage, 6.1 of them with the branch at its old price. With it the room is gone before a tile is added (the last tile lands at 418.4, with the last pair's down products begun at 416.7), which is why the eight tiles cost 21 in loads8, and why the function's gain is not to be found in the sum of the changed kernel.

**The second expert stage, -1: right** within its bounds at -0.3, in part by luck: a dearer branch was its bad case, and it came (4.4 for 1.4), but it hides a gain of the new function that was not foreseen and that branch_mixed shows (219.1 against 223.8).

**The faster rival** (no new waits) fell at 96.7. **The third**, that transfers take more back, was right in kind: the stage lost 11.9 instead of 7; retention itself lost 0.9, which is less than the executions differ by.
